# Values' and gates' weights and the gating norm's vectors issued behind the queries' and keys' transfers through DRAM

## The chip, the cores and the metric

The kernel runs on one core of a Trainium2 chip. The metric is the device time of one execution in microseconds (us). Five engines work side by side, each in its own order, and wait for one another by semaphores: TensorE (PE in the rows, its weight loads PEld), VectorE (DVE), ScalarE (ACT), GpSimd (POOL) and SyncE (SP), which here issues nearly all DMA transfers.

## What is computed

One layer of a hybrid decoder block on 256 tokens of width 1024: a SwiGLU feed-forward part, a mixing part with two branches and gates, and a second SwiGLU part, each with a norm ahead and added to the stream. The change lies in the mixing part:

```python
n = rmsnorm(h, mix_norm)
z = n @ w_in                               # 1024 -> 2560
q, k, v = z[..., :512], z[..., 512:1024], z[..., 1024:1536]
attn = moba_attention(q, k, v)             # 8 heads of 64; causal here, one block of 256 keys
zg = gelu(z[..., 1536:])
gm = chunked_spatial_gating(zg[..., :512], zg[..., 512:], ln_g, ln_b, w_s, b_s)
     # u * (W_s layernorm(v) + b), W_s lower triangular per group
gates = sigmoid(n @ w_gate + b_gate)       # 1024 -> 2048
h = h + (gates[..., :1024] * (attn @ w_branch_attn)
         + gates[..., 1024:] * (gm @ w_branch_gmlp)) @ w_out
```

## The kernel before

**Weights.** All weight matrices are cut into *units* of 1 MB, in the order in which TensorE wants them (`units`, L98 to L116): the queries `q`, keys `k`, the gating branch's second half `gv` and first half `u`, the values `v` (two units each), then eight units of gates. A unit is loaded in two halves of 512 KB by SP (`fetch_to`, L129) into a ring of seven buffers (`rawp`, `RAW`). For each half ScalarE makes a rounded copy (L193, CAST `w<-raw`) and VectorE the rest (L195, TENSOR_TENSOR `w<-raw,w`); three matmuls with these parts give the precision that is wanted (L188 to L190). The split parts of a unit lie in a ring of four (`wp`, `RING`). `unit(i, ahead)` (L154) splits everything up to `ahead` units beyond `i`, three in the mixing part's projections (`ALONE`), and then `fetch_to` issues loads for the seven halves that follow what is split. So a load is issued as soon as its buffer is free, some ten halves ahead of its matmuls.

**Order.** TensorE and SP follow the order in which the code is written, and within `in_order()` VectorE and ScalarE do too. Each DMA that SP issues has one of eight completion counters in rotation, and waits until the transfer that had this counter before it has landed. PSUM has eight banks, handed out in rotation (`bank`, L58).

**The stretch around the change** (L646 to L683). TensorE projects `q` (with the factors of the norm, L235), `k`, `gv` and `u`, each in two calls of `chunk` for the two units, 24 matmuls each; then come the scores (`scores`, L540, two calls with six banks in all), the spatial matmuls of the gating branch (`spatial`, L597, two banks), and the projection of `v`. Queries and keys have to be turned: `turn_qk` (L534) scales them on ScalarE and transposes squares of 32 x 32 on VectorE (L538); then SP writes them to DRAM by token (512 KB each, L650 and L654, `qkway<-mixed`) and reads them back in four transfers of 128 KB each (`from_way`, L360; `qback<-qkway` for the queries, `qk<-qkway` for the keys). The queries are put in order by a copy on ScalarE (L668); the keys are read by the scores as they arrive. Meanwhile `gv` goes through gelu (L662) and `layer_norm` (L634, twice, on VectorE with two small powers on GpSimd). The norm's vectors `ln_g` and `ln_b` (256 KB each, broadcast to all partitions) are loaded at L648 and L649. The result is what `spatial` reads. Scores are taken from PSUM by ScalarE (L558) and by VectorE with the mask added (L559).

Of the kernel before, what the change touches and what calls it, by code (L numbers as in the profile page):

```python
# [18 lines left out]
P = 128  # L19
# [10 lines left out]
GW = 512  # L30
# [7 lines left out]
RAW = 7  # L38
# [7 lines left out]
def block_kernel(ctx, tc, t, out):  # L46
    nc = tc.nc
# [10 lines left out]
    def bank(name):  # L58
        return psum.tile([P, 512], F32, tag="ps", name=name)
# [38 lines left out]
    units = []  # L98

    def add_units(name, n):  # L100
        first = len(units)
        units.extend((name, i) for i in range(n))
        return first
# [6 lines left out]
    mq, mk, mgv, mu, mv = (add_units(name, 2) for name in ("q", "k", "gv", "u", "v"))  # L110
# [7 lines left out]
    parts, raws = {}, {}  # L118
    fetched, done_to = [2 * FIRST], [2 * FIRST]

    def unit_tile(i):
        a, b = t[units[i][0]].shape[2:]
        parts[i] = wp.tile([P, a, 2, b], F32R, tag="w", name=f"w{i}")

    def half(i, hf):
        a = t[units[i][0]].shape[2]
        return slice(hf * a // 2, (hf + 1) * a // 2)

    def fetch_to(n):  # L129

        while fetched[0] < min(n, 2 * len(units)):
            i, hf = divmod(fetched[0], 2)
            fetched[0] += 1
            name, u = units[i]
            _, p, a, b = t[name].shape
            raws[i, hf] = rawp.tile([P, a // 2, b], F32, tag="raw", name=f"raw{i}_{hf}")
            nc.sync.dma_start(raws[i, hf], t[name][u][:, half(i, hf), :])

    def split_half(later=False):

        i, hf = divmod(done_to[0], 2)
        if hf == 0:
            unit_tile(i)
        fetch_to(done_to[0] + RAW)
        done_to[0] += 1
        w, sl = parts[i], half(i, hf)
        return split(w[:, sl, 0, :], w[:, sl, 1, :], raws.pop((i, hf)), later)
# [6 lines left out]
    def unit(i, ahead=PAIRED):  # L154
        split_to(i + 1 + ahead)
        return parts[i]
# [12 lines left out]
    def by_passes(sides, ks=range(KB), K=KB):  # L169


        for k in ks:
            if k < K - 1:
                for ps, of in sides:
                    (sh, _), both = of(k)
                    mm_high(ps, sh, both, k == 0, False)
        for k in ks:
            for ps, of in sides:
                (_, sl), both = of(k)
                mm_low(ps, sl, both)  # L180
        if K - 1 in ks:
            for ps, of in sides:
                (sh, _), both = of(K - 1)
                mm_high(ps, sh, both, False, True)

    def mm3(ps, st, mv_, first, last):
        (sh, sl), (mh, ml) = st, mv_
        nc.tensor.matmul(ps, sh, mh, start=first, stop=False)  # L188
        nc.tensor.matmul(ps, sh, ml, start=False, stop=False)  # L189
        nc.tensor.matmul(ps, sl, mh, start=False, stop=last)  # L190
# [7 lines left out]
    def alloc_T(name, tags):  # L198

        return [act.tile([P, 4, 2, S], F32R, tag=tag, name=f"{name}{c}") for c, tag in enumerate(tags)]  # L200
# [4 lines left out]
    def block_of(nT, k):  # L205
        return both_of(nT, k)[:, 0, :], both_of(nT, k)[:, 1, :]

    def in_order():

        return tc.manual_schedule(engines={mybir.EngineType.DVE, mybir.EngineType.Activation})  # L210
# [3 lines left out]
    def square(hh, pair, name, tag=None):  # L214

        if pair == 0:
            squares[name] = act.tile([P, KB, S], F32, tag=tag, name=f"sq{name}")
        two = slice(2 * pair, 2 * pair + 2)
        nc.scalar.activation(squares[name][:, two, :], hh[:, two, :], AF.Square, scale=D ** -0.5)

    def token_sums(name, engine=nc.vector):

        sq = squares[name]
        for n in (4, 2, 1):
            engine.tensor_add(sq[:, :n, :], sq[:, :n, :], sq[:, n:2 * n, :])

    def sum_parts(name):
        sq = squares[name]
        squares[name] = tmp.tile([P, 2, S], F32R, tag="hg", name=f"sqp{name}")
        split(squares[name][:, 0, :], squares[name][:, 1, :], sq[:, 0, :])  # L230
# [21 lines left out]
    def down_features(i0, n_units, both_of_k, scale, gain, nT, name, free, near, behind):  # L252

        acc = [bank(f"acc{name}{c}") for c in range(KB)]
        K = 2 * n_units

        def blocks(cs, ks):  # L260
            def of(c):
                def at(k):
                    w, sl = parts[i0 + k // 2], slice(c * P, (c + 1) * P)
                    return (w[:, k % 2, 0, sl], w[:, k % 2, 1, sl]), both_of_k(k)
                return at
            by_passes([(acc[c], of(c)) for c in cs], ks, K)

        far = n_units - near
        for i in range(far):
            unit(i0 + i, ALONE if i == far - 1 else PAIRED)  # L270

            for cs in ((range(KB - 2), range(KB - 2, KB)) if i == 0 else (range(KB),)):
                blocks(cs, (2 * i, 2 * i + 1))
            for then in behind[i:i + 1]:
                then()

        def low_part(c):
            hi, low = block_of(nT, c)
            nc.vector.scalar_tensor_tensor(low, h[:, c, :], gain[:, c:c + 1], hi.bitcast(F32),
                                           op0=ALU.mult, op1=ALU.subtract)  # L280

        lows = []
        for c in range(KB):
            blocks([c], range(2 * far, K))
            for q in range(2):
                nc.vector.scalar_tensor_tensor(h[:, c, :], acc[c][:, q * S:(q + 1) * S], scale, h[:, c, :],
                                               op0=ALU.mult, op1=ALU.add)
            nc.scalar.activation(block_of(nT, c)[0], h[:, c, :], AF.Identity, scale=gain[:, c:c + 1])  # L290
            if c:
                low_part(c - 1)
            if c in (4, KB - 1):
                lows.append(split_half(True))
            if c % 2:
                square(h, c // 2, name, free)
        low_part(KB - 1)
        for rest in lows:
            rest()
        token_sums(name)  # L300
        sum_parts(name)
# [43 lines left out]
    def chunk(i0, nT, name, c, us=range(2), ps=None):  # L345


        if ps is None:
            ps = [bank(f"{name}_{c}{j}") for j in range(NT)]
        for u in us:  # L350
            w = unit(i0 + 2 * c + u, ALONE)
            for k in range(4):
                for j in range(NT):
                    st = tuple(p[:, j * P:(j + 1) * P] for p in block_of(nT, 4 * u + k))
                    mm3(ps[j], st, (w[:, k, 0, :], w[:, k, 1, :]), u + k == 0, u == 1 and k == 3)
        return ps

    def from_way(to, way):

        squares32 = way.rearrange("(q r) a n -> r q a n", r=32)  # L360
        for a in range(4):
            nc.sync.dma_start(to[32 * a:32 * a + 32], squares32[:, :, a, :])

    def by_token(way):
        return way.rearrange("(j p) a n -> p j (a n)", p=P)
# [6 lines left out]
    class Hidden:  # L372
# [44 lines left out]
        def rest(self):  # L417

            last = NC // 2
            def first():  # L420
                self.leave(NC - 1)
                self.arrive(last - 1)
            return [first, lambda: self.settle(last - 1), lambda: self.arrive(last), lambda: self.settle(last)]
# [85 lines left out]
    nT2 = alloc_T("n2", ("nA", "nB"))  # L509

    with in_order():
        down_features(f1d, FB // 2, lambda k: hidden.aT[:, k], 0.5, gain2, nT2, "2", "nD", 2, hidden.rest())
        psq = chunk(mq, nT2, "q", 0)
        rs2 = token_factors("2")
        mixed = act.tile([P, 2 * FB, S], F32, tag="aT", name="mixed")
# [6 lines left out]
        gv, va, ut = tokens(mix_a[:, 16:20]), tokens(mix_b[:, 0:4]), tokens(mix_b[:, 4:8])  # L522
        lng, lnb = (mix[:, 20:22].rearrange("p a t -> p (a t)") for mix in (mix_a, mix_b))
# [121 lines left out]

        psk = chunk(mk, nT2, "k", 0, [0])  # L646
        turn_qk(0, psq)
        nc.sync.dma_start(lng, t["ln_g"].to_broadcast([P, GW]))  # L648
        nc.sync.dma_start(lnb, t["ln_b"].to_broadcast([P, GW]))  # L649
        nc.sync.dma_start(by_token(qk_way[0]), qk_turned[0])  # L650
        chunk(mk, nT2, "k", 0, [1], psk)
        turn_qk(1, psk)
        psgv = chunk(mgv, nT2, "gv", 0, [0])
        nc.sync.dma_start(by_token(qk_way[1]), qk_turned[1])  # L654
        q_back = tmp.tile([P, S // 32, P], F32, tag="back", name="qback", bufs=1)
        from_way(q_back, qk_way[0])
        chunk(mgv, nT2, "gv", 0, [1], psgv)
        qk = act.tile([P, 2, 4 * S], F32, tag="nC", name="qk")
        kT = qk[:, 1].rearrange("p (q c) -> p q c", q=S // 32)
        from_way(kT, qk_way[1])  # L660
        for j in range(NT):
            nc.scalar.activation(gv[:, j, :], psgv[j], AF.Gelu_apprx_tanh, scale=rs2[j])  # L662
        psu = chunk(mu, nT2, "u", 0, [0])
# [235 lines left out]
```

## Time and profile before

| | us |
|---|---|
| median of 3 runs | 530.01 |
| lowest and highest run | 526.02, 530.44 |
| the profiled execution | 530.29 |
| its span, first to last instruction | 528.6 |
| TensorE busy | 518.8 (98%) |
| VectorE busy | 357.3 (68%) |
| ScalarE busy | 265.1 (50%) |
| waits of TensorE for the returned keys | 2.2 |
| mean granted clock of TensorE | 0.993 |

Times in the rows count from the first instruction. A row of a timeline gives start, duration, engine, line, operation, what it writes and reads, how many instructions are merged, and in brackets the idle time ahead with what ended it. SPq rows are issues of transfers, whose duration is that of the issue alone; when a transfer lands is told by the chain and by the list of DMA issues. `PEclk` is the clock that TensorE was granted, as a share of full speed.

### The profile page before, as it was taken

What the parts mean: (1) busy time and instruction counts of PE and PEld (TensorE: products, weight loads), DVE (VectorE), ACT (ScalarE), POOL (GpSimd) and SP (SyncE); (2) the same over time, 40 slices, a digit from 0 to 9 for tenths busy, and PEclk for the clock granted to TensorE, in tenths of its full rate; (3) what the DMA queues carried; (4) which work ended last, traced back from release to release, by engine and by line L of the source; (5) the groups of instructions that cost most, each with busy time, mean ns of one, the idle gap of its engine ahead of it and who ended that gap; (6) DMA issues with size and microseconds to landing.
All of it is one profiled execution on the core that took longest, in us unless ns stands there. A gap on an engine that the chain in (4) does not pass through costs nothing.

```text
span 528.6 us, 6857 instructions
## 1 busy us (share of the span) xinstructions
PE 518.8 (98%) x2490; PEld 435.1 (82%) x2490; DVE 357.3 (68%) x501; ACT 265.1 (50%) x366; POOL 12.2 (2%) x20
## 2 busy tenths in 40 slices
PE   9999999999999999989999999999999999999995
PEld 7888888888888888868888898888888888888884
DVE  6886666675454689568976677988955765575424
ACT  7755354544344367548565423666544453463402
POOL 0010000000000001010000000001000000000002
PEclk9999999999999999989999999999999999999998
DMA  8999597988668229984799655829698889677302
GB/s 318 370 340 308 149 354 260 255 239 256 193 188 310 83 100 318 355 224 159 202 351 322 216 180 163 317 86 342 211 250 307 228 296 323 181 244 246 115 0 79
DMA packets 61937, 124.72 MB, mean 236 GB/s; under 512 B 11472, under 2 KB 35536, under 8 KB 61776
## 3 DMA queue, kind: packets, MB, share of 16 engines
q1 hardware_dynamic: 61616, 123.97, 72.4%
q8 instruction: 19, 0.31, 0.2%
q10 hardware_dynamic: 288, 0.33, 0.2%
q14 instruction: 14, 0.11, 0.1%
HBM read 112.21 MB, written 12.06 MB: 235 GB/s over the span
## 4 chain that ended last, share of the span: by engine, by line
PE 89%; DMA 5%; DVE 3%; issue 1%; ACT 1%; SPq 0%; POOLq 0%; DVEq 0%; POOL 0%; ACTq 0%
PE f L190 14%; PE f L188 14%; PE f L189 14%; PE acc L162 10%; PE acc L167 5%; PE acch L190 4%; PE acch L189 4%; PE acch L188 4%; PE g L188 3%; PE g L190 3%; PE g L189 3%; DVE w L195 2%; DMA qkway<-mixed 2%; DMA qk<-qkway 2%; DMA qback<-qkway 2%
## 5 line engine op out<-in xcount | busy, mean ns | idle before, releaser
L195 DVE TENSOR_TENSOR w<-raw,w 128x1024 fp32r<-128x1024 f32 x180 | 211.6, 1217 | 76.0 <-ACT w L193 75.9
L193 ACT CAST w<-raw 128x1024 fp32r<-128x1024 f32 x180 | 179.4, 1048 | 94.0 <-PE f L190 48.7
L190 PE MATMUL f<-w,n 128*128 128x512 f32 x336 | 130.7, 389 | 0.0
L188 PE MATMUL f<-w,n 128*128 128x512 f32 x336 | 130.7, 389 | 0.0
L189 PE MATMUL f<-w,n 128*128 128x512 f32 x336 | 130.7, 389 | 0.0
L189 PEld LDWEIGHTS f<-w,n 128*128 128x128 f32 x336 | 63.1, 188 | 13.2
L190 PEld LDWEIGHTS f<-w,n 128*128 128x128 f32 x336 | 63.1, 188 | 13.1
L188 PEld LDWEIGHTS f<-w,n 128*128 128x128 f32 x336 | 63.1, 188 | 12.9
L162 PE MATMUL acc<-f1h,w 128*128 128x512 f32 x176 | 43.4, 391 | 0.0
L162 PEld LDWEIGHTS acc<-f1h,w 128*128 128x128 f32 x176 | 31.9, 188 | 5.8
L188 PE MATMUL acch<-w,f2h 128*128 128x512 f32 x84 | 32.7, 389 | 0.0
L189 PE MATMUL acch<-w,f2h 128*128 128x512 f32 x84 | 32.7, 389 | 0.0
L190 PE MATMUL acch<-w,f2h 128*128 128x512 f32 x84 | 32.7, 389 | 0.0
L188 PE MATMUL g<-w,n 128*128 128x512 f32 x64 | 24.9, 389 | 0.0
L189 PE MATMUL g<-w,n 128*128 128x512 f32 x64 | 24.9, 389 | 0.0
L190 PE MATMUL g<-w,n 128*128 128x512 f32 x64 | 24.9, 389 | 0.0
L167 PEld LDWEIGHTS acc<-f1h,w 128*128 128x128 f32 x176 | 23.5, 191 | 1.5
L167 PE MATMUL acc<-f1h,w 128*128 128x256 f32 x176 | 23.9, 282 | 0.0
L387 ACT ACTIVATE f2s<-f,rstd 128x256 f32<-128x256 f32 x22 | 10.3, 473 | 27.2 <-PE f L190 27.0
L389 DVE SCALAR_TENSOR_TENSOR f2a<-f,rstd,f2s 128x256 f32<-128x256 f32 x22 | 10.2, 473 | 19.5 <-ACT f2s L387 19.5
L387 ACT ACTIVATE f1s<-f,rstd 128x256 f32<-128x256 f32 x22 | 10.3, 473 | 24.3 <-PE f L190 22.8
L188 PEld LDWEIGHTS acch<-w,f2h 128*128 128x128 f32 x84 | 15.8, 188 | 3.3
(172 smaller groups left out, 628.3 us busy)
## 6 DMA issues: line engine op xcount, KB each, us to landing
raw<-in_f SPq DMA_DIRECT2D x84, 512.0 KB, 6.2
raw<-in_f1d SPq DMA_DIRECT2D x22, 512.0 KB, 5.7
raw<-in_f2d SPq DMA_DIRECT2D x22, 512.0 KB, 6.4
raw<-in_gate SPq DMA_DIRECT2D x16, 512.0 KB, 8.1
raw<-in_out SPq DMA_DIRECT2D x8, 512.0 KB, 5.5
f1way<-f1t SPq DMA_DIRECT2D x11, 256.0 KB, 6.4
f2way<-f2t SPq DMA_DIRECT2D x11, 256.0 KB, 5.1
front<-in_first SPq DMA_DIRECT2D x7, 384.0 KB, 5.8
```

Source lines behind the costliest of these rows:

```text
L162: nc.tensor.matmul(ps, st, both.rearrange("p two n -> p (two n)"), start=first, stop=last)
L167: nc.tensor.matmul(ps[:, n:], st, both[:, 0, :], start=False, stop=False)
L188: nc.tensor.matmul(ps, sh, mh, start=first, stop=False)
L189: nc.tensor.matmul(ps, sh, ml, start=False, stop=False)
L190: nc.tensor.matmul(ps, sl, mh, start=False, stop=last)
L193: nc.scalar.copy(hi, src)
L195: nc.vector.tensor_sub(lo, src, hi.bitcast(F32))
L387: nc.scalar.activation(sg, ps[j][:, :CH], AF.Silu, scale=rs[j])
L389: nc.vector.scalar_tensor_tensor(a, ps[j][:, CH:], rs[j], sg, op0=ALU.mult, op1=ALU.mult)
```

## The change

```diff
@@ -118,6 +118,8 @@
     fetched, done_to = [2 * FIRST], [2 * FIRST]
 
+    hold = [None]
+
@@ -128,7 +130,7 @@
     def fetch_to(n):
 
-        while fetched[0] < min(n, 2 * len(units)):
+        while fetched[0] < min(n, hold[0] or n, 2 * len(units)):
@@ -510,6 +512,8 @@
         down_features(f1d, FB // 2, lambda k: hidden.aT[:, k], 0.5, gain2, nT2, "2", "nD", 2, hidden.rest())
+
+        hold[0] = 2 * mv
         psq = chunk(mq, nT2, "q", 0)
@@ -645,8 +649,6 @@
         psk = chunk(mk, nT2, "k", 0, [0])
         turn_qk(0, psq)
-        nc.sync.dma_start(lng, t["ln_g"].to_broadcast([P, GW]))
-        nc.sync.dma_start(lnb, t["ln_b"].to_broadcast([P, GW]))
         nc.sync.dma_start(by_token(qk_way[0]), qk_turned[0])
@@ -654,10 +656,14 @@
         from_way(q_back, qk_way[0])
-        chunk(mgv, nT2, "gv", 0, [1], psgv)
         qk = act.tile([P, 2, 4 * S], F32, tag="nC", name="qk")
         kT = qk[:, 1].rearrange("p (q c) -> p q c", q=S // 32)
         from_way(kT, qk_way[1])
+        nc.sync.dma_start(lng, t["ln_g"].to_broadcast([P, GW]))
+        nc.sync.dma_start(lnb, t["ln_b"].to_broadcast([P, GW]))
+        hold[0] = None
+        fetch_to(done_to[0] + RAW)
+        chunk(mgv, nT2, "gv", 0, [1], psgv)
```

While `hold` is set, no half from the first of `v` on is fetched. It is lifted behind the last read of the keys, and then seven halves are issued in one go: four of `v`, three of the gates. The norm's vectors stand ahead of them. The instructions of TensorE, VectorE, ScalarE and GpSimd and their order are the same as before.

SP's order in the kernel before, from the norm's vectors on to the reads of the keys (`raw` is the buffer of a half; `mixed` holds queries, keys and the norm's vectors in parts of one tile):

```order
L648 DMA mixed<-in_ln_g 128x512
L649 DMA mixed<-in_ln_b 128x512
L650 DMA qkway_1775<-mixed 128x2x512
L137 DMA raw_1_1822<-in_v 128x1024
L137 DMA raw_0_1826<-in_gate 128x1024
L137 DMA raw_1_1861<-in_gate 128x1024
L137 DMA raw_0_1865<-in_gate 128x1024
L654 DMA qkway_1776<-mixed 128x2x512
L362 DMA qback<-qkway_1775 32x8x128 x4
L137 DMA raw_1_1900<-in_gate 128x1024
L137 DMA raw_0_1904<-in_gate 128x1024
L362 DMA qk<-qkway_1776 32x8x128 x4
```

Three halves of `v` stand ahead of these rows. In the changed kernel the same place, directly behind the last half of `u`, reads:

```order
L652 DMA qkway_1773<-mixed 128x2x512
L656 DMA qkway_1774<-mixed 128x2x512
L364 DMA qback<-qkway_1773 32x8x128 x4
L364 DMA qk<-qkway_1774 32x8x128 x4
L662 DMA mixed<-in_ln_g 128x512
L663 DMA mixed<-in_ln_b 128x512
L139 DMA raw_0_1888<-in_v 128x1024
L139 DMA raw_1_1890<-in_v 128x1024
L139 DMA raw_0_1892<-in_v 128x1024
L139 DMA raw_1_1894<-in_v 128x1024
L139 DMA raw_0_1896<-in_gate 128x1024
L139 DMA raw_1_1898<-in_gate 128x1024
```

The ten transfers of queries and keys now stand together. The eleven loads that stood ahead of the keys' reads (four of `v`, the two vectors, five of the gates) all follow them. With the waits of SP beside them (DMAHW0 to DMAHW7 are the completion counters, Activation and DVE the engines that free a buffer), the rows of the changed kernel from the second read of the queries on are:

```order
L364 DMA qback<-qkway_1773 32x8x128 [waits DMAHW1_49]
L364 DMA qback<-qkway_1773 32x8x128 [waits DMAHW2_49]
L364 DMA qback<-qkway_1773 32x8x128 [waits DMAHW3_49]
L364 DMA qk<-qkway_1774 32x8x128 [waits DMAHW7_49,DMAHW4_49]
L364 DMA qk<-qkway_1774 32x8x128 [waits DMAHW5_49]
L364 DMA qk<-qkway_1774 32x8x128 x2
L662 DMA mixed<-in_ln_g 128x512 [waits DMAHW0_49,PE_49]
L663 DMA mixed<-in_ln_b 128x512 [waits DMAHW1_49]
L139 DMA raw_0_1888<-in_v 128x1024 [waits DMAHW2_49,Activation_49]
L139 DMA raw_1_1890<-in_v 128x1024 [waits DMAHW3_49,Activation_49]
L139 DMA raw_0_1892<-in_v 128x1024 [waits DMAHW4_49,Activation_49]
L139 DMA raw_1_1894<-in_v 128x1024 [waits DMAHW5_49,Activation_49]
```

The loads behind the keys' reads take over, one by one, the counters of the reads: the norm's vectors those of the first two reads of the queries, the first unit of `v` those of the last two, its second unit those of the first two reads of the keys. ScalarE's order is that of before; in the changed kernel's numbering, from the first half of `v` on:

```order
L195 CAST w_1902<-raw_0_1888 128x2x512
L195 CAST w_1902<-raw_1_1890 128x2x512
L668 ACT_TABLE_LOAD
L668 ACTIVATE mixed<-gv_1844,rstd_1766 128x512
L668 ACTIVATE mixed<-gv_1845,rstd_1766 128x512
L195 CAST w_1939<-raw_0_1892 128x2x512
L195 CAST w_1939<-raw_1_1894 128x2x512
L674 COPY qk<-qback 128x8x4x32
L195 CAST w_1993<-raw_0_1896 128x2x512
L195 CAST w_1993<-raw_1_1898 128x2x512
```

Nothing has moved here: the casts of `v`'s first unit stand ahead of the gelu of `gv`, those of its second unit ahead of the copy of the queries, and those of the first gate unit behind it. VectorE has the subtracts of `v`'s two units ahead of both layer norms, and those of the first gate unit between these and the first mask add.

## Rows read from the trace of the kernel before

**Rows 1.** The page, part 1: busy us, share of the span, instructions.

```profile
PE 518.8 (98%) x2490; PEld 435.1 (82%) x2490; DVE 357.3 (68%) x501; ACT 265.1 (50%) x366; POOL 12.2 (2%) x20
```

**Rows 2.** TensorE's waits behind its first matmul: us in total, times, longest us.

```profile
PE sc L552 <- DMA qk<-qkway: 2.2, 2, 1.7
```

**Rows 3.** Timeline of TensorE: start us, us, instruction, count, idle ahead.

```profile
230.41 0.39 PE L190 MATMUL u<-w,n 128*128 128x512 f32 x1
232.50 0.46 PE L552 MATMUL sc<-qk 64*128 64x128 f32 x2 [1.71 <-DMA qk<-qkway]
233.50 4.37 PE L552 MATMUL sc<-qk 64*128 64x128 f32 x30 [0.54 <-DMA qk<-qkway]
```

**Rows 4.** Windows: us, busy us (instructions) by engine, granted clock, DMA share, GB/s.

```profile
234.68:238.09 3.41, 3.41 (x16) 2.56 (x14) 2.03 (x5) 1.30 (x4) 0.00 (x0) 0.50 0.42 151
```

**Rows 5.** The chain that ended last, 205 to 240 us: start us, us, what.

```profile
207.66 8.74 DMA qkway<-mixed
...
216.84 8.06 DMA qback<-qkway
...
224.92 8.45 DMA qk<-qkway
...
237.87 2.10 PE mix L601 x16
239.97 0.23 PE v L188
```

**Rows 6.** Timeline of SP: start us, us for the issues, transfer, count.

```profile
201.93 3.94 SPq L137 DMA_DIRECT2D raw<-in_v  x3
...
206.40 1.16 SPq L649 DMA_DIRECT2D mixed<-in_ln_b  x1
...
216.47 2.07 SPq L362 DMA_DIRECT2D qback<-qkway  x4
...
223.28 1.93 SPq L362 DMA_DIRECT2D qk<-qkway  x4
```

**Rows 7.** DMA issues in four short stretches: count, KB each, median us to landing.

```profile
raw<-in_gv SPq DMA_DIRECT2D x1, 512.0 KB, 3.5
...
f1way<-f1t SPq DMA_DIRECT2D x1, 256.0 KB, 2.2
...
f1back<-f1way SPq DMA_DIRECT2D x4, 128.0 KB, 3.0
...
raw<-in_v SPq DMA_DIRECT2D x4, 512.0 KB, 8.4
```

**Rows 8.** Windows, as rows 4, during the store of the queries.

```profile
207.60:216.40 8.80, 8.80 (x41) 7.28 (x40) 6.30 (x7) 5.68 (x7) 0.00 (x0) 1.00 1.02 362
```

**Rows 9.** Timeline of ScalarE, columns as rows 3.

```profile
214.51 2.01 ACT L193 CAST w<-raw 128x1024 fp32r<-128x1024 f32 x2 [2.86 <-PE gv L190]
216.54 1.28 ACT L662 ACT_TABLE_LOAD   x1
219.27 1.37 ACT L662 ACTIVATE mixed<-gv,rstd 128x512 f32<-128x512 f32 x2 [1.45 <-PE gv L190]
...
226.40 1.05 ACT L668 COPY qk<-qback 128x1024 f32<-128x1024 f32 x1 [3.87 <-DMA qback<-qkway]
```

**Rows 10.** Timeline of VectorE, columns as rows 3.

```profile
205.71 1.31 DVE L538 STREAM_TRANSPOSE mixed<-mixed 128x512 f32<-128x512 f32 x2 [0.19 <-ACT mixed L537]
...
209.49 1.30 DVE L538 STREAM_TRANSPOSE mixed<-mixed 128x512 f32<-128x512 f32 x2
...
223.89 0.69 DVE L636 BATCH_NORM_STATS2 st<-mixed 128x6 f32<-128x512 f32 x1
...
228.96 0.75 DVE L644 SCALAR_TENSOR_TENSOR mixed<-mixed,lnr 128x512 f32<-128x512 f32 x1 [0.45 <-POOL lnr L642]
229.62 2.35 DVE L195 TENSOR_TENSOR w<-raw,w 128x1024 fp32r<-128x1024 f32 x2
...
234.47 1.29 DVE L559 TENSOR_TENSOR mixed<-sc,mask 128x512 f32<-128x512 f32 x2 [2.50 <-PE sc L552]
```

## The prediction

> **What bounds the kernel now.** I read the shares first: TensorE is busy 98% of the 528.6 us span [rows 1], so the kernel is as long as TensorE's list of matmuls plus its waits. The waits of TensorE come next: inside the kernel there is one place only, the scores (`sc`, L552), which wait 2.2 us for the keys coming back from DRAM [rows 2]. The timeline of TensorE shows it: the last matmul of `u` starts at 230.41, a matmul takes 0.23 of the queue, so the scores could start at 230.64; they start at 232.50 after 1.71 us idle, stop again for 0.54 us, and go on at 233.50 [rows 3]. Behind the two waits the granted clock is 0.50 (1.2 GHz) from 234.68 to 238.09 [rows 4]. That stretch holds scores and the spatial matmuls (`mix`), and half of 3.41 us, 1.7 us, is what it costs. `v` starts at 239.97 [rows 5].
>
> The chain says why the keys are late: three transfers in a row, 8.74 + 8.06 + 8.45 us [rows 5], all in one queue that runs at a DMA share of 1.02 meanwhile [rows 8]. The same kinds of transfer with little in front of them land in 3.5 us (512 KB load), 2.2 us (256 KB store) and 3.0 us (the 128 KB blocks) [rows 7]. So some 5 to 6 us of each of the three is queueing behind the values' and gates' weights.
>
> Without any wait and at full clock the scores need 3.2 us (0.46, and 4.37 less half of the 3.19 that lie in the slow stretch), `mix` 2.0, and `v` would start at 230.64 + 5.2 = 235.9. **The whole prize is 239.97 - 235.9 = 4.1 us**, 0.8% of the time.
>
> **The change, part by part.** No instruction is added or removed, and the order on TensorE, VectorE and ScalarE is that of before; only SP's queue is rearranged.
>
> *Queries and keys.* The queries' transposes end at 205.71 + 1.31 = 207.0 and the keys' at 209.49 + 1.30 = 210.8 [rows 10]. These become the issue times of the two stores (207.66 before for the queries' [rows 5]). With a clear queue I price a 512 KB store like the lone 512 KB load, 3.5 us; below lies the lone 256 KB store at 2.2, above the 8.74 of before. It is nearest to the load, since it has the same bytes. Queries land in DRAM at 210.6, keys at 214.3. The four reads of the queries take SP 2.07 us to issue, those of the keys 1.93 [rows 6], so the keys' reads are issued from 214.3 to 216.2 and land by 216 + 3.0 = 219. The scores want them at 230.6: this wait is gone with 11 us to spare, and with the early bound by more. Even at the contended prices of before (210.8 + 8.74 + 1.93 + 8.45 = 229.9) they would be in time.
>
> *What is late next: the values' weights.* Before, their first half was issued at 201.93 [rows 6]; now SP reaches the norm's vectors at 216.2 and, at 0.5 us (a quarter of 2.07) to 1.16 us an issue [rows 6], the two halves of the first unit of `v` at about 217.2 and 217.7. The completion counters add nothing here by my times: `v`'s halves take the counters of the queries' last and the keys' first reads, which have landed or are about to. Let T be the landing of the second of these halves: 217.7 + 3.5 alone, + 1.8 because a megabyte (two vectors and the first half) is issued just ahead of it, 2.9 us of transfer at 362 GB/s [rows 8] of which 1.5 is past by 217.7, and 0.4 for the tail of the keys. T = 223.0. Lower bound 221.2 (nothing ahead); upper bound 226.1 with the 8.4 us that `v`'s halves took before [rows 7].
>
> ScalarE has the casts of these halves *ahead* of the gelu of `gv`, the casts of `v`'s second unit, and the copy of the queries [rows 9]; before, they ran at 214.51. From T on, in ScalarE's and then VectorE's order: second cast 1.0, table 1.3, two gelus 1.4, two casts 2.0 (as the pair at 214.51) [rows 9], last subtract 1.2, both layer norms 5.8 (223.89 to 229.71), two subtracts of the first gate unit 2.36, first mask add 0.65 [rows 10]. The queries' copy ends at T + 1.0 + 1.3 + 1.4 + 2.0 + 1.05 = 229.8, before TensorE is done with `u`. So the scores run from 230.64 to 233.9 without a wait. The layer norms end at T + 12.7 = 235.7; `mix` reads their result, so TensorE waits 1.8 us and has `mix` done at 237.7. `v` takes the two PSUM banks of the first scores (six banks for scores and two for `mix` make up the eight), and these come free with the mask add, at T + 15.7 = 238.7. TensorE waits 1.0 more.
>
> **Sum.** `v` starts at T + 15.7 = 238.7 and not at 239.97: -1.3 us, if no slow stretch of the clock falls on it. The break-even is T = 224.3. For the bounds of T the sum is -3.1 and +1.8. What the clock does I take from the one place that shows it: 1.7 + 0.5 us of waiting cost 1.7 us. Now 1.8 + 1.0 us of waiting stand some 3 us later, in two pieces about 2 us apart. If the clock falls on `mix` alone, which waits anyway, it costs about 1; if on `v`, 1.7, and the sum is +0.4. I take no fall for the likeliest, and keep both.
>
> After that VectorE is some 1.6 us later than before (its mask adds start at 238.1 and not at 234.47, but it waited between them before) while TensorE is 1.3 us earlier. TensorE has no wait on VectorE anywhere else [rows 2], and I cost this at nothing; what hides it is the distance at which weights are split ahead, three units. Without that cover the price would be at most the 2.9 us between them. The next halves on the queue, `v`'s second unit and the first of the gates, are 2 MB more, 5.8 us at 362 GB/s: `v`'s by T + 2.9 = 225.9, for casts that ScalarE reaches at T + 3.7, and the gates' by T + 5.8 = 228.8, for casts that it reaches at 229.8. They fit, the last by a microsecond.
>
> The profiled execution took 530.29 us (span 528.6, 1.7 around it): 530.29 - 1.3 = **529.0 us**. Its median is 530.01, so on that footing it is 528.7; the runs of before spread from 526.02 to 530.44, more than the prize. About 1% (5.3 us) is what a measurement of this kernel can tell from no change.
>
> **Rivals.** (a) *All is hidden.* T at or below 221.5, if stores and blocks land faster than the load: -2.8 to -4.1, 526.2 to 527.5. For it: the blocks of 64 and 128 KB and the lone store are quick [rows 7]. Against: even T = 221.2 leaves `v` at 236.9. Chance 0.18.
>
> (b) *Slower: the weights of `v` take the keys' place as the late transfer.* Place: ScalarE's cast at the head of the chain above. From T = 224.3 the kernel is slower, a microsecond for each. With 8.4 us a load it is +1.8 (532.1), with a fall of the clock 533.8; if every transfer keeps its old price, keys in DRAM are there at 219.5, the reads issued at 221.4, the second half at 222.9, T = 231.3, and it is +7.0: 537.3. For it: everything that `v` needs is now serial behind the keys, in one queue. Against: the 8 us of before are queueing, and there is nothing ahead but the transfers counted. Chance 0.28, of which 0.07 beyond +1%.
>
> The rows show `v`'s loads issued at 201.93 [rows 6], 12.6 us ahead of their cast at 214.51 [rows 9]; the change cuts that lead to about 5 us. A rule of the Trainium skill speaks for (b) here: its page "DMA: Bandwidth & Descriptors", section "Rules for kernel authors", says to issue a DMA early, compute, and wait for it late. By that rule the loads should stay early, and the time would be that of (b), 532 to 537; whether the trace agrees is open, as the rows of before have no load with a short lead.
>
> (c) *The change does nothing measurable to the keys*, because other work slows these transfers: then the keys still arrive by 229.9 and the price is that of (b)'s end; it is counted there.
>
> **How the numbers follow.** Forecast 0.50 (its own range 527.5 to 530.8: T from 221.5 to 224 without a fall of the clock, or about 223 with one), (a) 0.18, (b) 0.28, and 0.04 for something that I don't see. The range of 8 in 10 takes in most of (a) and the mild part of (b): 526.0 to 532.6. Since the prize is 4.1 us, faster by over 1% has 0.03, slower by over 1% 0.07, within 1% 0.90.
>
> **What would show it.** Right: no wait of `sc` on `qk<-qkway`; the store of the queries and of the keys landing in 3 to 4 us; ScalarE waiting before the cast of `v`'s first unit until about 222 to 223; small waits of `mix` on VectorE's layer norm and of `v` on the mask add. Wrong: those casts ready well before 221 (then (a)), or after 225 (then (b)); SP standing at the issue of `v` for the keys' reads longer than a microsecond; waits of TensorE past 250, which I cost at nothing; another slow stretch of the clock.

## The result, and the profile after

The changed kernel is a little slower: 531.85 us (median of 11 executions, 531.09 to 533.41) against 528.91 us for the kernel before in the same comparison (11 executions, 526.02 to 530.93). The ratio is 1.0062, with a 95% interval of 1.0039 to 1.0084. The forecast was 529.0, a gain of 1.3 us: the sign was wrong, the time lies inside the range of 526.0 to 532.6, and what happened is rival (b).

The executions of the kernel before scatter: most take between 525.8 and 529.5 us and about a fifth (5 of 11, 4 of 29, 6 of 23 and none of 17 in the four series taken beside the changed kernel and those below) between 529.6 and 531.8, and the execution profiled ahead of the prediction (530.29) is one of these.

The span of the profiled execution of the changed kernel is 530.7 us (532.47 in all, granted clock 0.995). The page's part 1, as [rows 1], shows the same work:

```profile
PE 518.9 (98%) x2490; PEld 435.3 (82%) x2490; DVE 356.8 (67%) x501; ACT 264.0 (50%) x366; POOL 12.2 (2%) x20
```

The waits of TensorE in the changed kernel, columns as [rows 2]:

```profile
PE mix L605 <- DVE mixed L648: 3.4, 1, 3.4
PE warm L94 <- DVE zeros L91: 1.2, 1, 1.2
PE acc L164 <- DVE mixed L740: 0.6, 1, 0.6
PE f L468 <- ACT n L444: 0.3, 1, 0.3
```

The wait of the scores for the keys, 2.2 us before, is gone. In its place the spatial matmuls wait 3.4 us for the layer norm on VectorE. Two small waits stand elsewhere: 0.3 us at the very start of the kernel (L468, at 5.3 us) and 0.6 us some 80 us later, in the merge of the two branches (L164).

SP's queue shows why. Timeline of SP in the changed kernel, to be held against [rows 6]:

```profile
207.47 0.38 SPq L652 DMA_DIRECT2D qkway<-mixed  x1
211.26 0.38 SPq L656 DMA_DIRECT2D qkway<-mixed  x1
211.74 2.38 SPq L364 DMA_DIRECT2D qback<-qkway  x4
214.59 1.78 SPq L364 DMA_DIRECT2D qk<-qkway  x4
216.47 0.39 SPq L662 DMA_DIRECT2D mixed<-in_ln_g  x1
216.91 0.43 SPq L663 DMA_DIRECT2D mixed<-in_ln_b  x1
217.44 2.31 SPq L139 DMA_DIRECT2D raw<-in_v  x4
```

The stores go out at 207.47 and 211.26 and the eight reads from 211.74 to 216.4, nearly as forecast, and the values' weights at 217.44 and 217.91. How long they took, from the DMA issues between 207 and 223 us (count, KB each, median us from issue to landing), against [rows 7]:

```profile
raw<-in_v SPq DMA_DIRECT2D x4, 512.0 KB, 7.2
...
qkway<-mixed SPq DMA_DIRECT2D x2, 512.0 KB, 3.0
qback<-qkway SPq DMA_DIRECT2D x4, 128.0 KB, 3.9
qk<-qkway SPq DMA_DIRECT2D x4, 128.0 KB, 4.2
```

The stores fell from the 8.74 of [rows 5] to 3.0, and the reads from some 8 us to about 4. But the weights of the values still took 7.2 (median of four halves; those of the first unit took 6.0 and 6.8), and they now start 15.5 us later than before. The timeline of ScalarE, to be held against [rows 9], shows their landing, since the casts start as soon as the halves are there:

```profile
210.10 1.99 ACT L195 CAST w<-raw 128x1024 fp32r<-128x1024 f32 x2
223.56 1.05 ACT L195 CAST w<-raw 128x1024 fp32r<-128x1024 f32 x1 [11.47 <-DMA raw<-in_v]
224.77 1.05 ACT L195 CAST w<-raw 128x1024 fp32r<-128x1024 f32 x1 [0.15 <-DMA raw<-in_v]
225.84 1.28 ACT L668 ACT_TABLE_LOAD   x1
227.13 1.27 ACT L668 ACTIVATE mixed<-gv,rstd 128x512 f32<-128x512 f32 x2
228.29 2.00 ACT L195 CAST w<-raw 128x1024 fp32r<-128x1024 f32 x2
230.18 1.05 ACT L674 COPY qk<-qback 128x1024 f32<-128x1024 f32 x1
```

ScalarE stands 11.47 us for the first half and is at the second at 224.77; the gelus of `gv` (L668), which [rows 9] have at 219.27, start at 227.13. VectorE takes the lateness on (its timeline, against [rows 10]):

```profile
231.64 0.69 DVE L640 BATCH_NORM_STATS2 st<-mixed 128x6 f32<-128x512 f32 x1
...
236.70 0.75 DVE L648 SCALAR_TENSOR_TENSOR mixed<-mixed,lnr 128x512 f32<-128x512 f32 x1 [0.45 <-POOL lnr L646]
237.36 2.35 DVE L197 TENSOR_TENSOR w<-raw,w 128x1024 fp32r<-128x1024 f32 x2
239.63 2.61 DVE L563 TENSOR_TENSOR mixed<-sc,mask 128x512 f32<-128x512 f32 x6
```

The layer norm starts at 231.64 and not at 223.89, its last operation (L648) at 236.70 and not at 228.96, and the first mask add at 239.63 and not at 234.47. TensorE, against [rows 3]:

```profile
231.28 2.96 PE L556 MATMUL sc<-qk 64*128 64x128 f32 x32
237.59 2.73 PE L605 MATMUL mix<-mixed,wsT 128*128 128x128 f32 x16 [3.35 <-DVE mixed L648]
240.37 0.80 PE L190 MATMUL v<-w,n 128*128 128x512 f32 x1
```

The scores run through in one piece, `mix` waits 3.35 us, and `v` starts at 240.37. In the profiled execution of before this view has:

```profile
239.73 0.48 PE L188 MATMUL v<-w,n 128*128 128x512 f32 x1
```

And the clock falls again, later than in [rows 4] (windows, columns as there):

```profile
238.72:242.14 3.42, 3.36 (x13) 2.78 (x12) 3.42 (x7) 0.00 (x0) 0.00 (x0) 0.50 0.62 181
215.70:220.36 4.66, 4.66 (x22) 3.88 (x21) 0.00 (x0) 0.00 (x0) 0.00 (x0) 1.00 1.12 213
220.40:229.90 9.50, 9.50 (x43) 7.88 (x42) 2.97 (x3) 6.16 (x7) 0.00 (x0) 1.00 1.01 394
```

The first row is at half clock (1.2 GHz). It covers the end of `mix` and 1.77 us of `v` (240.37 to 242.14), and half of that is lost. The second row is the landing of the eight reads, with the DMA engines counted as full (share 1.12) at only 213 GB/s; the third, the two vectors (landed at 221.49 and 222.16) and then weights, runs at 394 GB/s. The slow landing of the reads is the term that the forecast made too small.

Span against span (530.7 - 528.6 = 2.1 us) the pieces are: 0.44 from ahead of the stage (`u` starts at 220.19, before at 219.75), 0.20 for `v` (240.37 - 239.73 - 0.44), 0.8 for the slow clock on `v` (up to the first matmul of the gates, 252.18 against 250.73, the delay has grown to 1.45 us), and 0.7 in the merge, where `f` of the second feed-forward follows at 344.41 against 342.22. From there to the end the delay stays at 2.2.

### The profile page after: what moved, and what is told of

The parts are those of the page before. It is cut to its first block, busy times and chain, and to the rows that moved or that the text cites. A ratio compares the mean times of both kernels' runs of the same rounds, so it can differ in the third digit from the quotient of the medians.

```text
span 530.7 us, 6854 instructions
## 1 busy us (share of the span) xinstructions
PE 518.9 (98%) x2490; PEld 435.3 (82%) x2490; DVE 356.8 (67%) x501; ACT 264.0 (50%) x366; POOL 12.2 (2%) x20
## 4 chain that ended last, share of the span: by engine, by line
PE 83%; DVE 6%; DMA 4%; issue 3%; ACT 2%; SPq 1%; POOL 0%; POOLq 0%; DVEq 0%; ACTq 0%
PE f L192 14%; PE f L191 14%; PE f L190 14%; PE acc L164 10%; PE acc L169 5%; PE acch L192 4%; PE acch L191 4%; PE acch L190 4%; DVE w L197 3%; PE g L191 3%; PE g L192 3%; PE g L190 3%; DMA raw<-in_v 1%; ACT w L195 1%; SPq L364 1%
## 5 line engine op out<-in xcount | busy, mean ns | idle before, releaser
L164 PE MATMUL acc<-f1h,w 128*128 128x512 f32 x176 | 43.4, 391 | 0.0
L164 PEld LDWEIGHTS acc<-f1h,w 128*128 128x128 f32 x176 | 31.9, 188 | 5.8
```

Of the source, the lines that this page charges most:

```text
L164: nc.tensor.matmul(ps, st, both.rearrange("p two n -> p (two n)"), start=first, stop=last)
```

## The experiments

The theory that came out of this reading is called A: the values' first unit (two halves of 512 KB) lands after the break-even, and since its casts stand ahead of the gelu of `gv` on ScalarE, all that `mix` and `v` need comes late. The rivals put the loss elsewhere. In the expectations B stands for the weight stream being late as a whole, whatever waits for it (in e5: each late megabyte counts), and C for the layer norm waiting for the norm's late vectors. D came up after the first runs: in most executions of before the keys are just in time, so there was little to win.

All of the timed runs stand beside runs of the kernel before on the same chip, and the ratios below are to these. A difference between medians of two kernels from different series is looser: the changed kernel's median lies 4.4 us above that of e1, 1.5 above e3 and 2.2 below e4, and by the ratios to before it is 3.4, 1.3 and 2.8. To make the profiles comparable I count from the first matmul of `u` and list the start of `v` and of the second feed-forward's first `f` behind it (differences of starts in the timelines of TensorE, of the one profiled execution):

| kernel | median, us | profiled execution, us | `v` after `u` | `f` after `v` |
|---|---|---|---|---|
| before, first profile | 528.91 | 530.29 | 19.98 | 102.49 |
| changed | 531.85 | 532.47 | 20.18 | 104.04 |
| e1 values' first unit early | 527.44 | 526.87 | 15.60 | 103.20 |
| e2 casts behind | 527.04 | 527.08 | 15.60 | 103.82 |
| e3 vectors early | 530.37 | 532.45 | 19.84 | 104.93 |
| e4 a megabyte more ahead | 534.02 | 535.12 | 23.77 | 103.60 |
| e0 before, second profile | | 526.44 | 15.60 | 102.54 |
| e0 before, third profile | | 526.60 | 15.81 | 102.93 |
| e5 gates and vectors held | 526.75 | 526.76 | 15.60 | 103.37 |
| e6 vectors alone | 530.09 | 531.12 | 19.43 | 103.90 |
| e7 gates alone held | 526.59 | 526.42 | 15.60 | 103.10 |

15.60 is what this stretch takes when TensorE waits for nothing in it.

**e1: only the values' first unit goes early.** This is the changed kernel with one number changed, so that the hold begins one unit later:

```
-        hold[0] = 2 * mv
+        hold[0] = 2 * mv + 2
```

> The change, but the first unit of v (two halves) is not held back: it is loaded ahead of the stores, as before; the second unit, the gates and the norm's vectors stay behind the keys' reads. Theory A (the loss is the late landing of v's first unit, at whose casts ScalarE stands with the gelu of gv and the copy of the queries behind it): the casts run at about 215 again, mix has no wait, v starts at about 236.3 where it started at 240.4; time 526 to 527.5, below both kernels. Rival B (the loss is the whole weight stream being 10 us late, felt later too): four fifths of the stream are still late, so 531 to 532. Rival C (the layer norm waits for the late vectors): the vectors are as late as in the change, so 531 to 532 and VectorE waits at L647 for the DMA.

Measured: 527.44 us (526.87 to 528.43, 12 executions) against 527.24 for before; ratio 0.9997 (0.9979 to 1.0014). TensorE in e1, timeline:

```profile
230.96 2.89 PE L556 MATMUL sc<-qk 64*128 64x128 f32 x32
233.78 2.05 PE L605 MATMUL mix<-mixed,wsT 128*128 128x128 f32 x16
235.59 0.47 PE L190 MATMUL v<-w,n 128*128 128x512 f32 x1
```

No wait is left, neither for the keys (their last read lands at 219.61) nor for the layer norm, and no half clock. One megabyte issued earlier takes 4.4 us off the changed kernel's median and 4.6 us off its way from `u` to `v`. A holds. That e1 would also be below the kernel before did not come true: this is where D begins.

**e2: the loads as late as in the change, their casts behind the gelu.** The casts of the two units of `v`, and of the first gate unit behind them, are asked for one unit later in the program (`PAIRED` is two units ahead, `ALONE` three). On ScalarE the casts of `v`'s first unit then stand behind the gelu of `gv`, and those of its second unit behind the copy of the queries:

```
-    def chunk(i0, nT, name, c, us=range(2), ps=None):
+    def chunk(i0, nT, name, c, us=range(2), ps=None, ahead=ALONE):
...
-            w = unit(i0 + 2 * c + u, ALONE)
+            w = unit(i0 + 2 * c + u, ahead)
...
-        chunk(mgv, nT2, "gv", 0, [1], psgv)
+        chunk(mgv, nT2, "gv", 0, [1], psgv, PAIRED)
...
-        psu = chunk(mu, nT2, "u", 0, [0])
+        psu = chunk(mu, nT2, "u", 0, [0], None, PAIRED)
...
-        chunk(mu, nT2, "u", 0, [1], psu)
+        chunk(mu, nT2, "u", 0, [1], psu, PAIRED)
```

> The change, with all loads as late as it makes them, but three projections (second unit of gv, both of u) split two units ahead and not three, so that ScalarE has the gelu of gv ahead of the casts of v's first unit, and the copy of the queries ahead of those of the second. Theory A: the weights still land at about 224.7, but nothing that TensorE needs stands behind them; layer norms end by 233, mix has no wait, v starts at 236 to 237; time 526 to 528. Rival B (late stream as such): no gain, 531 to 532.

Measured: 527.04 us (526.46 to 529.43, 12 executions); ratio 0.9993 (0.9974 to 1.0013). Timeline of ScalarE in e2:

```profile
219.11 1.37 ACT L668 ACTIVATE mixed<-gv,rstd 128x512 f32<-128x512 f32 x2 [6.32 <-PE gv L192]
222.83 1.05 ACT L195 CAST w<-raw 128x1024 fp32r<-128x1024 f32 x1 [2.35 <-DMA raw<-in_v]
224.06 1.05 ACT L195 CAST w<-raw 128x1024 fp32r<-128x1024 f32 x1 [0.17 <-DMA raw<-in_v]
225.01 1.05 ACT L674 COPY qk<-qback 128x1024 f32<-128x1024 f32 x1
```

Counted from `u`, the second cast starts at +4.47 here and at +4.58 in the changed kernel: the halves come as late as there. But the gelus run at 219.11, ahead of them, and `v` starts at 15.60. So the lateness of the transfer costs nothing by itself; it costs because the gelus, and with them the layer norm and `mix`, stand behind the waiting cast on an engine that takes its instructions in order.

**e3: the norm's vectors early again.** The changed kernel, with the two loads of the vectors put back ahead of the queries' store:

```
         turn_qk(0, psq)
+        nc.sync.dma_start(lng, t["ln_g"].to_broadcast([P, GW]))
+        nc.sync.dma_start(lnb, t["ln_b"].to_broadcast([P, GW]))
         nc.sync.dma_start(by_token(qk_way[0]), qk_turned[0])
...
-        nc.sync.dma_start(lng, t["ln_g"].to_broadcast([P, GW]))
-        nc.sync.dma_start(lnb, t["ln_b"].to_broadcast([P, GW]))
         hold[0] = None
```

> The change, but the norm's two vectors are issued ahead of the stores, as before. Theory A: half a megabyte less stands ahead of v's first unit, which lands 1.3 to 1.8 us earlier, and v starts as much earlier; time 530 to 530.6 against 531.9. Rival C (the vectors themselves are waited for): the whole loss is gone, 527 to 529. Rival B: unchanged, 531.5 to 532.

Measured: 530.37 us (528.80 to 532.45, 12 executions); ratio 1.0038 (1.0018 to 1.0059), the median is 1.5 us under that of the changed kernel. Waits of TensorE in its profile:

```profile
PE mix L605 <- DVE mixed L648: 3.2, 1, 3.2
PE acc L164 <- DVE mixed L740: 1.4, 2, 0.7
```

The profiled execution is the slowest of its twelve, so it understates the gain: in it the second half of the values' first unit lands at 223.83, which counted from `u` is only 0.35 us sooner than in the change, and `v` is sooner by 0.34. Chain and landing move together; `v` starts 15.64 us after that landing, in the changed kernel 15.63. By the medians the half megabyte of the vectors is a part of the loss, and the smaller one.

**e4: a megabyte more ahead of the values.** The load of the gates' bias (1 MB, broadcast) is moved from where it stood, 20 lines below, to directly ahead of the end of the hold:

```
+        nc.sync.dma_start(gates[:, 0, :], t["b_gate"].to_broadcast([P, 2 * D]))
         hold[0] = None
...
-        nc.sync.dma_start(gates[:, 0, :], t["b_gate"].to_broadcast([P, 2 * D]))
```

> The change, with the 1 MB load of the gates' bias moved from behind the first unit of v's projection to directly ahead of the held weights: nothing is needed from it until 265 us. Theory A: v's first unit lands 2.6 us later (two transfers of 1.3), and v starts as much later, by a microsecond for each; time 534 to 535. Rivals B and C: within 0.5 us of the change, 531.5 to 532.4.

Measured: 534.02 us (533.53 to 535.24, 6 executions); ratio 1.0116 (1.0087 to 1.0145). The values' second half lands at 227.21, counted from `u` 3.0 us later than in the change (7.52 against 4.55); `v` starts 3.6 us later (23.77 against 20.18) and the median is 2.2 us up: roughly a microsecond for a microsecond, the slope that rival (b) gives. The waits of TensorE and the slow stretches (windows) in e4:

```profile
PE sc L556 <- ACT qk L675: 3.0, 1, 3.0
PE mix L605 <- DVE mixed L648: 2.0, 1, 2.0
```

```profile
233.21:236.62 3.41, 2.88 (x22) 2.84 (x24) 2.90 (x6) 3.41 (x5) 0.99 (x1) 0.50 0.89 316
240.03:243.45 3.42, 3.38 (x16) 3.41 (x17) 3.42 (x5) 1.82 (x2) 0.00 (x0) 0.50 0.38 102
```

Now even the scores wait, not for the keys from DRAM but for ScalarE's copy of them, which stands behind the same late casts, and the clock falls twice.

**e0: the kernel before, profiled twice more.** No edit. If e1 has neither wait and is not faster than before, then before should mostly not have the wait of [rows 2] either.

> The kernel before once more, for another profiled execution. The forecast was made against an execution of 530.3 us; others of the same kernel take 526 to 528. Theory D: those differ in the waits of the scores and in what the clock does behind them: this execution, if it takes 526 to 528, has no stretch at half clock behind the scores, and a wait of at most 2.2 us. Rival: the waits are those of the first profile and the difference lies in another stage.

> As the run above, a third execution of the kernel before: 526 to 528 without the slow stretch of the clock, or about 530 with it.

Measured: 526.44 and 526.60 us, spans 524.7 and 524.9. TensorE in the first of them has one wait in all, and its timeline in this stretch is that of e1:

```profile
PE warm L94 <- DVE zeros L91: 1.2, 1, 1.2
```

```profile
231.23 2.89 PE L552 MATMUL sc<-qk 64*128 64x128 f32 x32
234.05 2.05 PE L601 MATMUL mix<-mixed,wsT 128*128 128x128 f32 x16
235.86 0.47 PE L188 MATMUL v<-w,n 128*128 128x512 f32 x1
```

The DMA issues of the same execution, for the keys' reads (columns as above):

```profile
qk<-qkway SPq DMA_DIRECT2D x4, 128.0 KB, 7.2
```

The keys still queue for 7.2 us. But their last block lands at 231.05 and in the third profile at 230.90, with the scores starting at 231.23 and 230.78: just in time. In the profile ahead of the prediction it landed at 233.36; counted from `u` that is 13.61, against 10.79 and 11.09. Why the queue ran 2.5 to 2.8 us later in that execution was not tried and stays open. D holds for three profiles: two have no wait of the scores and half the clock nowhere in this stretch, one has both. Between e0 and the changed kernel, execution against execution, lie 6.0 us of span: 4.6 from `u` to `v`, and 1.5 behind it, of which 0.8 is the slow clock on `v` and 0.7 the merge (less 0.1 ahead of `u`).

**e5: gates' weights and vectors held, the values early.** As e1, with both units of the values ahead of the hold:

```
-        hold[0] = 2 * mv
+        hold[0] = 2 * mv + 4
```

> The change, but no half of v is held back, only the gates and the norm's vectors. Theory A: v's first unit is cast at about 215, and the keys, now behind two megabytes of v, still land by 223, seven us early; no wait of scores or of mix: 526.5 to 527.5, as when only the first unit is let through. Rival B (each late megabyte counts): clearly below that run, 525 to 526.

Measured: 526.75 us (526.38 to 528.56, 12 executions) against 527.43 (525.77 to 531.77, 23 executions); ratio 0.9975 (0.9947 to 1.0002). The keys land at 222.03, 8.7 us ahead of the scores (230.72), and `v` is at 15.60. It is the best ratio of the study, and its interval just includes no change.

**e6: the vectors alone.** The kernel before, with only the two loads of the vectors moved behind the keys' reads:

```
-        nc.sync.dma_start(lng, t["ln_g"].to_broadcast([P, GW]))
-        nc.sync.dma_start(lnb, t["ln_b"].to_broadcast([P, GW]))
         nc.sync.dma_start(by_token(qk_way[0]), qk_turned[0])
...
         from_way(kT, qk_way[1])
+        nc.sync.dma_start(lng, t["ln_g"].to_broadcast([P, GW]))
+        nc.sync.dma_start(lnb, t["ln_b"].to_broadcast([P, GW]))
```

> The kernel before with one part of the change: only the norm's vectors move behind the keys' reads; nothing is held. The keys come some 1.3 us earlier (half a megabyte less ahead). The vectors are issued at about 224 behind eight transfers and land at 232 to 233, and the layer norms, which began at 224 to 225, wait for them: v starts at 240.5 to 241. By theory A (what stands ahead of the layer norm in its engine's order decides) 529 to 531, with VectorE waiting for the DMA of the vectors; if the vectors' place is indifferent, 526 to 527.

Measured: 530.09 us (527.54 to 533.28, 10 executions); ratio 1.0044 (1.0013 to 1.0075). The execution profiled took 531.12, so the wait below is that of one of the longer ones. VectorE in e6, timeline:

```profile
231.30 0.75 DVE L643 SCALAR_TENSOR_TENSOR mixed<-mixed,mvr 128x512 f32<-128x512 f32 x1 [6.35 <-DMA mixed<-in_ln_g]
```

With the weights still early the queue is full, the vectors land at 231.27 and 231.94, and the layer norm waits 6.35 us for them. In the changed kernel they land at 221.49 and 222.16, 11 us before they are read (L647 at 232.65, L648 at 233.83). So the vectors hurt in two ways: behind a full queue by their own landing, behind an empty one by the time that they take from the values.

**e7: only the gates' weights wait.** The vectors early as in e3 and the hold as in e5; what is left of the change is that the gates' weights go behind the keys.

> The kernel before with one part of the change alone: the gates' weights wait for the keys' reads; v's halves and the norm's vectors keep their places ahead of them. The keys have no gates in front and land by about 223 to 224, seven us before the scores; nothing that ScalarE or VectorE reads before the scores is late. By theory A and D: no wait of scores or of mix, 526 to 527.5 in every execution, so the executions of about 530 that the kernel before has are gone (largest below 529), and the median is 0.5 to 1 us below it. If the executions of 530 have another cause than the keys, some of twelve will show it here too.

Measured: 526.59 us (525.97 to 528.88, 12 executions) against 526.90 (526.02 to 529.45, 17 executions); ratio 0.9996 (0.9981 to 1.0011). The keys land at 222.48 and TensorE waits for nothing in the stretch. A gain of 0.5 to 1 us was expected and 0.3 was measured, which is none that can be told. Its executions end at 528.88 and e5's at 528.56, where before had some above 529.6 in three of four series; but before had none above 529.45 on the chip of e7, so that the slow executions are gone is likely and not shown.

## Why the prediction was wrong

*The keys and queries.* Right in kind. The stores took 2.8 us (207.47 to 210.25) and 3.3 us (to 214.52), priced at 3.5 each; the scores don't wait for the keys. The keys' last read lands at 220.36, forecast 219: of no weight for the scores, but see the next step.

*The landing of the values' first unit.* This is the step that failed: the term T was mis-sized, and with it the whole gain of 1.3 us is gone. Forecast 223.0; measured 224.74, or 224.3 without the 0.44 us by which this execution is late from the start: just the break-even, to which the clock and the later stages then add. The issue was right (217.91 for the second half, forecast 217.7), but the forecast put 5.3 us behind it and it took 6.83. The failed piece is "0.4 for the tail of the keys". The eight reads, 128 KB each, land one every 0.67 us from 215.70 to 220.36, which is 196 GB/s; the last lands 2.45 us after the values' second half is issued. The 4.9 us for what comes behind the tail (1.4 left of the megabyte, 3.5 for the half) measured 4.38 (220.36 to 224.74), so the tail alone is too small. The prediction's own times were at odds here: with the keys landed at 219 and the half issued at 217.7 the tail is 1.3. The 3.0 us of [rows 7] was the delay of four such blocks in a quiet stretch; what counts for the load behind them is how long eight in a row hold the queue, and that I had not worked out. The upper bound that I kept, 226.1, held it.

*The chain from T to `v`.* Right to 0.1 us: 240.37 - 224.74 = 15.63, forecast 15.7, though composed of ten rows of before. Here a chain on in-order engines could be added up from rows of another place; the landing behind a mixed queue could not.

*The clock.* I took no fall for the likeliest and kept a fall on `v` as +0.4 for the sum. It fell, over the end of `mix` and the start of `v`, and cost 0.8 us on `v`. With T at the break-even, 0.2 for `v` (the forecast took its start before from the chain, 239.97, where the timeline has 239.73) and this 0.8 make +1.0 in the stretch, where -1.3 was forecast.

*The prize.* "The whole prize is 4.1 us" was the second step that failed, and no view of the first profile could show it. It is right for the execution profiled (19.98 - 15.60 = 4.4 us), but e0 has next to nothing of it in two profiles (15.60 and 15.81), and e1, e2, e5 and e7, which remove the wait for the keys without a new one in this stretch, come out between 0.2 above and 0.7 us below before in the median. The text set the sum against 530.29 and noted that the runs spread from 526.02 to 530.44, "more than the prize"; it should have asked whether that spread was the prize itself. Against an execution without the wait, with `v` 15.60 us behind the start of `u` (219.75) and the chain of 15.63 from T, the break-even is T = 219.7, and even the lower bound of 221.2 is a loss.

*Past 250 us.* "I cost this at nothing" was short by 0.7 us: TensorE waits 0.64 us in the merge for VectorE (L740). By the trace the token blocks that went through DRAM came back later by 0.7 us than the delay of the rest (ScalarE's cast of them, behind a wait for that transfer, at 320.28 against 318.09, less 1.45). All changed kernels show such a wait, of 0.5 to 1.4 us, also those in which `v` is at 15.60, and before shows 0, 0 and 0.3. So it isn't the lateness of VectorE that I had weighed; why these transfers land later was not tried and stays open.

*The rivals.* (b) was given 0.28; with a fall of the clock it had 533.8 at 8.4 us a load, and without one 532.1. The loads took 6.0 and 6.8 us. (a) did not happen, nor did (c): the keys were there at 220.36 and not at 229.9. Of the rule that the Trainium skill's page "DMA: Bandwidth & Descriptors" gives under "Rules for kernel authors", to issue a DMA early and wait for it late, the prediction left open whether the trace agrees. It does as far as time goes: e1, with the first unit issued early, takes 527.44 and the changed kernel 531.85. e2, 527.04, says where it ends: the same late loads cost nothing once no other work stands behind their casts.

## What to carry to other kernels

Profile a kernel that scatters by as much as a wait is worth more than once before that wait is taken for the prize: here one profile in three had it. When loads are held back for a critical transfer, hold only those whose first consumer comes after what the transfer feeds (here the gates' weights, not the values'; and even that, e7, gained nothing that can be told), and look on each in-order engine at what stands behind that consumer. Price a queue by what is still in flight when the load is issued, small blocks by their own measured rate and not by that of large ones.

## What the runs showed of the hardware

Blocks of 128 KB read back from DRAM landed every 0.67 us, 196 GB/s, while the DMA engines counted as full (share 1.12); the vectors and weights behind them ran at 394 GB/s with a share of 1.01. A full share alone does not tell the rate. What makes these blocks slow was not tried. With no weights ahead in the queue the time from issue to landing of such a block was 3.8 to 4.4 us, where [rows 7] have 3.0; the first of them was issued at 211.74, just behind the keys' store, which landed at 214.52.

The granted clock fell to 0.50 (1.2 GHz) at or behind every longer wait of TensorE seen in this stretch: 3.35 us in the changed kernel, 3.2 us in e3, 2.2 us in e6, 3.0 and 2.0 us in e4, and the two pieces of 1.71 and 0.54 us of [rows 3]. It fell between 0.5 us ahead of the end of the wait (e4, 233.21 against 233.74) and 1.2 us behind it ([rows 4]). The windows of e3 and of e6, columns as above:

```profile
237.63:241.04 3.41, 3.41 (x14) 2.94 (x13) 3.41 (x8) 0.01 (x1) 0.00 (x0) 0.50 0.58 169
236.08:239.50 3.42, 3.42 (x17) 3.42 (x17) 3.42 (x6) 1.35 (x2) 0.00 (x0) 0.50 0.40 122
```

In e1, e2, e5, e7 and both profiles of e0, which don't wait there, it did not. So a late landing costs more than its own wait: keys that landed 2.5 to 2.8 us later in the first profile of before than in e0 put `v` 4.2 to 4.4 us later. `v` stands at 15.60 or 15.81, or at 19.43 and above, and in nine kernels and eleven profiles nowhere between.
